# Another placement in SBUF, product f of the output projection in three passes, and a new order for a decoder layer on one core

## The chip, the cores and the metric

The kernel runs on one core of one Trainium2 chip. The metric is the device time of one execution in microseconds (us). The kernel before the change took 919.77 to 920.34 us in three runs, median 920.08. One further execution was profiled; it took 918.02 us, of which the profile's span covers 916.3.

TensorE (PE) does the matmuls: one operand is loaded into the array ("loaded", 128 x 128), the other runs through it ("streamed", 256 or 512 columns), and the result goes to a bank of PSUM. PEld is the weight load, which the profile counts apart. DVE (VectorE) and ACT (ScalarE) do the arithmetic on the vectors, POOL (GpSimd) and SP (SyncE) only start transfers here.

## The reference

One layer on 512 positions of width 1024, in float32:

```
h = rmsnorm(x)
p = h @ w_in                       # 1024 x 9216: B, C, v | a, b | queries | 3 gates
y_a = (B * conv3(C * v)) @ w_a_out
y_b = silu(layernorm(conv31(a * sigmoid(b)))) @ w_b_out
y_c = attention(queries, 256 memory tokens: K, V = rmsnorm(mem) @ w_kv) @ w_att_out
m   = sum_i sigmoid(gate_i) * y_i
x   = x + m @ w_o
x   = x + (silu(g) * up) @ w_down  # g, up = split(conv3(rmsnorm(x) @ w_up)), 2816 each
out = rmsnorm(x)
```

## The kernel before

**Precision.** Every large product is made of float32r matmuls. Each operand is split into a high part (a cast to float32r, on ACT: `whi`, `mgh`, ...) and a low part (what is left, a subtraction on DVE: `wlo`, `mgl`, ...), and three passes are added up in PSUM: high x high, high x low, low x high. Product f of the output projection (`wo_whole`, L2076) is the exception: it runs as eight full float32 matmuls on unsplit operands, which the trace records as 16.

**Quads.** The projections by `w_in`, by `w_att_out` and by `w_up` are done by a seven-product scheme on 2 x 2 blocks of 256 columns. A quad `(q, f)` is product f of group q: 24 matmuls of 256 columns (2 column halves x 4 k x 3 passes), written by `multiply` (L882). The groups are `glu` (a, b), `q`, `gate`, `cv` (C, v), `bb` (B), `mo` (attention output), `mq` and `up`. The loaded operand is the weight part, the streamed one the activation's `form`. For `mo` the streamed operand lies among the general places `lf` and `sb`, for the other groups that the prediction times in the `forms` pool. K is a quad of its own kind (`keys_product`, L1242). V, the output projection (`wo`, products a to g, of which a, b and d use weight parts held in the `forms` pool) and the down-projection (`pd`) go through `product` (L650 to L652), 512 columns each; the merge of branch b (L1832 to L1834) streams 512 columns of activations.

**Blocked matmuls.** In some quads one matmul, the first, walks its 256 columns in another order, in blocks of 16 columns taken from the two halves alternately (a "blocked" matmul, shown as `128x2x8x16`; in some `up` quads with f = 7 the block is 64, 16 or 8). Its result is the same. It stands in a quad that follows a product of 512 columns, in the listed quads of the set `FRESH`, and in these `up` quads: 35 quads in all, five of them with blocks of 64 or 8.

**Places.** SBUF holds weight parts (`wts` pool: `whi`, `wlo`, four pairs), six landing places for weights (`wf`), 6 general places `lf` from the left, 17 general places `sb` from the right, and the pool `forms`. Each place is 4096 bytes per partition. `SHIFT` is a tile of 192 bytes at the head of `forms`, so the forms start 192 bytes further than they would. The addresses that the pools give, modulo 512: weight parts 256, `lf` 256, `sb` 256, `forms` 448. The difference between the address of the streamed and of the loaded operand, modulo 512, is called the distance below: 192 in the quads whose operand is in `forms`, 0 in those of `mo`.

**Order.** A planner (`Jobs`) takes each engine's instructions as jobs with a cost, what they wait for, and what place they take. `ORDER` fixes the order of TensorE's 363 jobs. All others are put in order by due time: the time when the TensorE job that needs them is to start, less their length, plus a number by kind of job (`LATER`). `AHEAD` bounds how early a kind may run. A place is taken when free; a low part by DVE, the next addition on POOL, a landing of a weight, each follows from a due time.

**Loads.** Weights of a quad come by SP in plain transfers of 512 KB; four of the seven combinations are made by POOL transfers that add a second block onto the first as it lands. 162 such transfers run through POOL's queue.

Of the kernel before, what the change touches and what calls it, by code (L numbers as in the profile page):

```python
# [80 lines left out]
LATER = {  # L81
    "ACT c3": -1610.2, "ACT cf": -759.4, "ACT csq": -104.7, "ACT exp": -604.9,
# [29 lines left out]
    "ACT xg": 3.7, "ACT xroot": -520.5, "ACT xsq": -264.1, "ACT xsquare": -849.4,  # L112
    "ACT zh a": -212.1, "ACT zh b": -569.9, "ACT zh c": 46.3, "ACT zh d": -1022.4,
    "ACT zh e": 465.7, "ACT zh f": 365.1, "ACT zh g": -370.3, "DVE CV": -750.2, "DVE c3": -619.6,
    "DVE cf": -1.8, "DVE csum": -1543.8, "DVE ends": -15.4, "DVE fl h b00": -12.9,
# [20 lines left out]
    "DVE s6 glu": -216.7, "DVE sl": -459.1, "DVE sum": 477.6, "DVE tap 0": 173.9,  # L136
    "DVE tap 1": 446.5, "DVE tap 2": 252.4, "DVE tap 3": -27.1, "DVE top": -1718.1,
    "DVE tot1": -7.6, "DVE tot2": 42.7, "DVE um": 169.1, "DVE v scale": -86.8,
    "DVE var fold": -637.8, "DVE vl": 915.9, "DVE weigh": -3786, "DVE wl K 0": -119.6,
# [2617 lines left out]
```

## Time and profile before

| what | value |
|---|---|
| median of three runs | 920.08 us (919.77 to 920.34) |
| the profiled execution | 918.02 us |
| span of its profile | 916.3 us |
| TensorE busy | 906.6 us, 6930 records |
| DVE busy | 852.3 us, 954 instructions |
| ACT busy | 709.8 us, 992 instructions |
| POOL busy | 141.8 us, 169 instructions |
| DMA | 199.55 MB, mean 218 GB/s |

A line of engine waits gives engine, waiting instruction, what it waited for, total us, number and mean. A window gives start and end in us from the span's start, its length, then the busy time of each engine and the instructions that touch the window, the granted TensorE clock as a share of full speed, the mean busy share of the DMA engines, and GB/s. In the chain of waits a row is start, length and instruction. Dividing a window that holds only whole matmuls of one kind by their number gives the time of one.

### The profile page before, as it was taken

The numbers are of one execution on the slowest core, as the hardware profiler recorded it, in microseconds if no ns is written. First come the engines' busy times: TensorE is split into PE (matmuls) and PEld (weight loads), VectorE is DVE, ScalarE is ACT, GpSimd is POOL, SyncE is SP. The second block draws the span as 40 slices with busy tenths as digits, with TensorE's granted clock in tenths as the row PEclk, the third lists the DMA queues.
The fourth block names the chain that finished last, engine by engine and source line by source line (L and its number), as shares of the span: only waits on it lengthen the run. The fifth ranks groups of instructions, "written<-read, shape, count | busy, mean of one in ns | idle before, by whom it ended". The sixth has DMA issues, their size and how long they took to land.

```text
span 916.3 us, 17357 instructions
## 1 busy us (share of the span) xinstructions
PE 906.6 (99%) x6930; PEld 864.2 (94%) x6930; DVE 852.3 (93%) x954; ACT 709.8 (77%) x992; POOL 141.8 (15%) x169
## 2 busy tenths in 40 slices
PE   9999999999999999999999999999999999999997
PEld 8899999999999999999899997899999999988886
DVE  6997999999999999999999989897898799999987
ACT  7867989979969878799958974686777668865556
POOL 0120211011121111101111112112211211002120
PEclk9999999999999999999999999999999999999999
DMA  9998689877799869979777999999998956779972
GB/s 371 355 244 202 136 200 202 237 161 176 136 247 210 198 157 211 225 176 215 175 154 206 212 277 336 226 230 299 281 259 205 236 134 150 181 263 327 266 144 93
DMA packets 56129, 199.55 MB, mean 218 GB/s; under 512 B 6240, under 2 KB 6640, under 8 KB 56048
## 3 DMA queue, kind: packets, MB, share of 16 engines
q0 software_dynamic: 23328, 84.16, 50.5%
q1 hardware_dynamic: 32544, 114.02, 34.7%
q8 instruction: 54, 0.88, 0.4%
q10 hardware_dynamic: 176, 0.27, 0.1%
q14 instruction: 27, 0.22, 0.1%
HBM read 194.23 MB, written 4.19 MB: 217 GB/s over the span
## 4 chain that ended last, share of the span: by engine, by line
PE 95%; DVE 3%; ACT 1%; issue 1%; DVEq 0%; ACTq 0%
PE bank L882 67%; PE bank L652 6%; PE bank L650 6%; PE bank L651 6%; PE bank L1242 2%; PE bank L1833 2%; PE bank L1834 2%; PE bank L1832 2%; PE bank L2076 1%; DVE wlo L703 1%; PE bank L1111 1%; PE bank L2246 0%; PE bank L1231 0%; DVE x L2625 0%; DVE x L2604 0%
## 5 line engine op out<-in xcount | busy, mean ns | idle before, releaser
L699 ACT CAST whi<-wf 128x1024 fp32r<-128x1024 f32 x210 | 217.7, 1044 | 59.4 <-PE bank L882 32.4
L703 DVE TENSOR_TENSOR wlo<-wf,whi 128x1024 fp32r<-128x1024 f32 (+1 forms) x207 | 249.1, 1212 | 13.4 <-ACT whi L699 12.7
L1576 ACT ACTIVATE tp<-u,pk 128x510 f32<-128x510 f32 (+22 forms) x184 | 120.4, 708 | 10.5 <-DVE acc L1583 8.2
L1583 DVE TENSOR_TENSOR acc<-acc,tp 128x964 f32<-128x964 f32 (+22 forms) x92 | 109.1, 1188 | 2.7 <-ACT tp L1576 0.7
L824 POOL DMA_DIRECT2D wf<-in_w_in x52 | 47.6, 941 | 226.0 <-DVE wlo L703 180.4
L882 PE MATMUL bank<-ft4h,whi 128*128 128x256 f32 x248 | 68.8, 277 | 0.9 <-DVE V L656 0.9
L882 PE MATMUL bank<-ft6h,whi 128*128 128x256 f32 x248 | 68.9, 278 | 0.5 <-ACT bank L955 0.5
L882 PE MATMUL bank<-ft7h,whi 128*128 128x256 f32 x248 | 68.8, 277 | 0.0
L882 PE MATMUL bank<-fb11l,whi 128*128 128x256 f32 x248 | 68.7, 277 | 0.0
L882 PE MATMUL bank<-fb11h,whi 128*128 128x256 f32 x248 | 68.7, 277 | 0.0
L882 PE MATMUL bank<-fb10h,whi 128*128 128x256 f32 x248 | 68.6, 277 | 0.0
L882 PE MATMUL bank<-fb11h,wlo 128*128 128x256 f32 x248 | 68.6, 277 | 0.0
L882 PE MATMUL bank<-ft7l,whi 128*128 128x256 f32 x248 | 68.6, 277 | 0.0
L882 PE MATMUL bank<-ft4l,whi 128*128 128x256 f32 x248 | 68.6, 277 | 0.0
L882 PE MATMUL bank<-ft6l,whi 128*128 128x256 f32 x248 | 68.6, 277 | 0.0
L882 PE MATMUL bank<-ft6h,wlo 128*128 128x256 f32 x248 | 68.6, 277 | 0.0
L882 PE MATMUL bank<-ft4h,wlo 128*128 128x256 f32 x248 | 68.6, 277 | 0.0
L882 PE MATMUL bank<-ft7h,wlo 128*128 128x256 f32 x248 | 68.6, 277 | 0.0
L882 PE MATMUL bank<-fb00h,whi 128*128 128x256 f32 x248 | 68.6, 277 | 0.0
L882 PE MATMUL bank<-fb00l,whi 128*128 128x256 f32 x248 | 68.6, 277 | 0.0
L882 PE MATMUL bank<-ft5h,whi 128*128 128x256 f32 x248 | 68.6, 277 | 0.0
L882 PE MATMUL bank<-ft5l,whi 128*128 128x256 f32 x248 | 68.6, 277 | 0.0
(427 smaller groups left out, 3220.9 us busy)
## 6 DMA issues: line engine op xcount, KB each, us to landing
wf<-in_w_in SPq DMA_DIRECT2D x56, 512.0 KB, 5.0
wf<-in_w_in POOLq DMA_DIRECT2D x52, 512.0 KB, 7.5
wf<-in_w_up POOLq DMA_DIRECT2D x33, 512.0 KB, 7.2
wf<-in_w_up SPq DMA_DIRECT2D x29, 512.0 KB, 8.1
wf<-in_w_down SPq DMA_DIRECT2D x15, 512.0 KB, 4.6
wf<-in_w_v SPq DMA_DIRECT2D x8, 512.0 KB, 9.5
wf<-in_w_a_out SPq DMA_DIRECT2D x8, 512.0 KB, 5.7
wf<-in_w_b_out SPq DMA_DIRECT2D x8, 512.0 KB, 4.8
```

What stands on the lines that cost most here:

```text
L650: nc.tensor.matmul(ps, s_hi, w_hi, start=start, stop=False, skip_group_check=again)
L651: nc.tensor.matmul(ps, s_hi, w_lo, start=False, stop=False, skip_group_check=again)
L652: nc.tensor.matmul(ps, s_lo, w_hi, start=False, stop=stop, skip_group_check=again)
L699: nc.scalar.copy(parts[0], src())
L703: nc.vector.tensor_tensor(lo, src(), hi.bitcast(F32), op=ALU.subtract)
L824: nc.gpsimd.dma_start(out=tiles[key], in_=block(w, col[c], k), accum_op=ALU.add)
L882: nc.tensor.matmul(to, w[:, k, at], col, start=first and n == 0, stop=k == 3 and n == 2, skip_group_check=again,)
L1242: nc.tensor.matmul(ps[:, j, :], w[:, k, at], a[:, k, :], start=first and j == 0 and k == 0 and n == 0, stop=g == 1 and k == 3 and n == 2, ...
L1576: nc.scalar.activation(two(("tp", p, s))[:, j, s:], two(("u", p))[:, j, : SEQ - s], AF.Copy, scale=weight(j),)
L1583: nc.vector.tensor_tensor(a, a, two(("tp", p, s))[:, :, s:], op=ALU.add)
L1832: nc.tensor.matmul(ps, w_hi[:, i, at], hi, start=first, stop=False)
L1833: nc.tensor.matmul(ps, w_hi[:, i, at], lo, start=False, stop=False)
```

## The change

Six things are changed together.

1. `WO_WHOLE` is empty: product f runs as 24 float32r matmuls of 512 columns instead of eight full ones, with split operands. The program has 16 more matmuls in it and six more jobs on other engines: three casts on ACT, three subtractions on DVE.
2. The 192-byte `SHIFT` tile now heads the `lf` pool, which lies left of `forms`, so both move; `mean_col`'s tile has 72 floats instead of 56, so `sb` lies 64 bytes lower. Modulo 512 the addresses now are: weight parts 256, `lf` 448, `sb` 192, `forms` 448. The distances of the forms' quads (192) and of V (320) stay. Counting float32r matmuls by distance, the others go: `mo` (336) from 0 to 192 (160) and 448 (176); merge (192) from 0 to 192 (80) and 448 (112); the down-projection's 429 of 512 columns and 66 of 256 columns from 0 to 320; attention scores (96 of 256 columns) 40 from 0 to 256; attention output (48 of 512 columns) 36 from 0 to 256; `wo` products c, e and g (72) from 0 to 64, a, b and d (72) from 192 to 256, and f comes in at 64.
3. `LEFT_SLOTS` is 9 instead of 6. The room comes from `dynamic_dma_scratch_size`, set to 4096 bytes; before it was 16384.
4. `FRESH` is empty, and a new set `STEADY` has four quads, in which the blocked matmul is the seventh (`nth = 6`) instead of the first. Blocked matmuls stand in 23 quads in the first place and in 4 in the seventh.
5. `ORDER`, `LATER` and `AHEAD` have new numbers; in `ORDER` there is no job that was not there before, nor is one missing.
6. A new table `NUDGE` of 565 numbers moves single jobs' due times.

```diff
-WO_WHOLE = "f"
+WO_WHOLE = ""
...
-LEFT_SLOTS, RIGHT_SLOTS = 6, 17
+LEFT_SLOTS, RIGHT_SLOTS = 9, 17
...
 FRESH = {
-    (("glu", 0), 2), (("glu", 3), 5), (("glu", 3), 3), (("cv", 1), 4), (("cv", 3), 6),
-    (("bb", 1), 4), (("mq", 1), 3), (("up", 0), 6), (("up", 0), 4), (("up", 2), 6),
+
+}
+NUDGE = {
+    'ldg': -5.5, 'mfold': 227.1, 'mfold2': 36.7, 'msum': -190.7, 'rm': -137.3, 'temps': 1.2,
...
+STEADY = {
+    ('K', 2, 0), (('gate', 1, 0), 2), (('gate', 1, 0), 3), (('up', 1), 2),
 }
...
-                due[key] += LATER.get(self.kind(key), 0.0)
+                due[key] += LATER.get(self.kind(key), 0.0) + NUDGE.get(key, 0.0)
...
-    mean_col = edge.tile([P, 56], F32, tag="mean_col", name="mean_col")[:, :1]
+    mean_col = edge.tile([P, 72], F32, tag="mean_col", name="mean_col")[:, :1]
     places = {"lf": ctx.enter_context(tc.tile_pool(name="lf", bufs=1, reuse_waits="tile"))}
+    places["lf"].tile([P, SHIFT // 4], F32, tag="shift", name="shift")
     forms_pool = tc.tile_pool(name="forms", bufs=1, reuse_waits="tile")
     forms = forms_pool.__enter__()
-    forms.tile([P, SHIFT // 4], F32, tag="shift", name="shift")
...
-        run = None
-        if long_rows(seq[seq.index((q, f)) - 1]) or (q, f) in FRESH:
+        run, nth = None, 0
+        if (q, f) in STEADY:
+            run, nth = 16, 6
+        elif long_rows(seq[seq.index((q, f)) - 1]) or (q, f) in FRESH:
             run = 16
...
-                    if run is not None and (c, k, n) == (0, 0, 0):
-                        to, col = blocks(to), blocks(col)
+                    if run is not None and (c, 3 * k + n) == (0, nth):
+                        to, col = in_blocks(to, run), in_blocks(col, run)
...
+                    to, col = ps[:, j, :], a[:, k, :]
+                    if ("K", h, g) in STEADY and (j, 3 * k + n) == (0, 6):
+                        to, col = in_blocks(to, 16), in_blocks(col, 16)
...
-    nc = bacc.Bacc("TRN2", target_bir_lowering=False, num_devices=1)
+    nc = bacc.Bacc(
+        "TRN2", target_bir_lowering=False, num_devices=1, dynamic_dma_scratch_size=4096
+    )
```

The order of the instructions, at the places that the prediction speaks of. In a row, the name left of the arrow is the bank or tile that is written, the names right of it are what is read, then the shape that is streamed; "x2" is the same row twice.

TensorE in the output projection, before: one product is ending, product f stands as a full-precision pair, and the next begins (`who` parts are held weights, `mg` the merged activations).

```order
L650 MATMUL bank_6780<-whoh_6531,mgh_6593 128x512
L651 MATMUL bank_6780<-whol_6532,mgh_6593 128x512
L652 MATMUL bank_6780<-whoh_6531,mgl_6597 128x512
L2076 MATMUL bank_6799<-wo_6301,mg_6703 128x512 x2
L650 MATMUL bank_6776<-whoh_6633,mgh_6593 128x512
L651 MATMUL bank_6776<-whol_6634,mgh_6593 128x512
L652 MATMUL bank_6776<-whoh_6633,mgl_6597 128x512
```

The same place now:

```order
L830 MATMUL bank_6833<-whoh_6707,mgh_6532 128x512
L831 MATMUL bank_6833<-whol_6708,mgh_6532 128x512
L832 MATMUL bank_6833<-whoh_6707,mgl_6561 128x512
L830 MATMUL bank_6856<-whi_6703,mgh_6844 128x512
L831 MATMUL bank_6856<-wlo_6704,mgh_6844 128x512
L832 MATMUL bank_6856<-whi_6703,mgl_6849 128x512
```

Product f (bank 6856) now comes after products a and b and as three passes on parts `whi`, `wlo`, `mgh`, `mgl`.

DVE around the same place, before (L703 makes low parts of weights, L2010 and L1917 the merged activations):

```order
L2010 TENSOR_TENSOR mg_6703<-mg_6773,mg_6703 128x1024
L1917 TENSOR_TENSOR mg_6458<-g_2654,g_5777 128x512
L703 TENSOR_TENSOR whol_6796<-wo_6705,whoh_6795 128x1024
L656 SCALAR_TENSOR_TENSOR mg_6567<-mg_6703,mg_6567 128x1024
L1093 TENSOR_TENSOR wo_6705<-wo_6705,wo_6301 128x1024
```

Now:

```order
L2195 TENSOR_TENSOR mg_6743<-mg_6816,mg_6743 128x1024
L2290 TENSOR_TENSOR x_856_6676<-x_856_6676,bank_6787 128x512
L836 SCALAR_TENSOR_TENSOR mg_6596<-mg_6743,mg_6596 128x1024
L2217 TENSOR_TENSOR mgl_6849<-mg_6743,mgh_6844 128x1024
L2290 TENSOR_TENSOR x_869_6783<-x_869_6783,bank_6791 128x512
L883 TENSOR_TENSOR whol_6823<-wo_6741,whoh_6822 128x1024
```

The low part of product f's activations (`mgl_6849`, L2217) is a new row behind the sum it is made from; the low parts of its weights stand some twenty rows ahead.

TensorE at K behind the squares of the memory tokens, before: two one-column matmuls, then plain ones of 256 columns.

```order
L1242 MATMUL bank_204<-mh_127,wlo_174 128x256
L1105 MATMUL ss_247<-mean_col,msq_161 128x1 x2
L1242 MATMUL bank_252<-mh_127,whi_235 128x256
L1242 MATMUL bank_252<-ml_128,whi_235 128x256
L1242 MATMUL bank_252<-mh_127,wlo_236 128x256
```

Now the seventh matmul of that quad is blocked:

```order
L1287 MATMUL ss_247<-mean_col,msq_161 128x1 x2
L1427 MATMUL bank_252<-mh_127,whi_235 128x256
L1427 MATMUL bank_252<-ml_128,whi_235 128x256
L1427 MATMUL bank_252<-mh_127,wlo_236 128x256
...
L1427 MATMUL bank_252<-mh_127,whi_235 128x2x8x16
```

Nothing moved there but the shape of one matmul.

More of the change, by code (lines that the diff above doesn't have):

```diff
@@ L103 @@
-    "ACT tap 1": -527.4, "ACT tap 2": -125.6, "ACT tap 3": -47.1, "ACT tp 0": 7.1, "ACT tp 1": 1965,
[8 rows of a table removed]
[L112 to L115, printed above, removed]
[8 rows of a table removed]
-    "DVE kl": -1303.6, "DVE kt": -2.5, "DVE lns": -829.6, "DVE low": -328.6, "DVE m scale": -946.8,
@@ L125 @@
-    "DVE mfold": 247.7, "DVE mfold2": -512, "DVE mg0": 302.6, "DVE mgl a": 1211, "DVE mgl b": 76.2,
-    "DVE mgl c": -546.6, "DVE mgl d": -216.3, "DVE mgl e": -277.9, "DVE ml": 845.8,
[9 rows of a table removed]
[L136 to L139, printed above, removed]
[6 rows of a table removed]
@@ L146 @@
-    "DVE wsum": -13.9, "DVE x scale": -264.1, "DVE x1 a": -77.5, "DVE x1 c": -156.8,
-    "DVE x1 d": -145.7, "DVE x1 e": -1579.6, "DVE x1 f": -689.2, "DVE x1 g": 224.3, "DVE xfold": 44,
-    "DVE xn": 566.3, "DVE xnorm": -43.3, "DVE xsum": -375.3, "DVE y t4": 108.1, "DVE y t5": -139.1,
[3 rows of a table removed]
-    "NONE c3": -8.5, "NONE cf": 768.4, "NONE first tile": 4.9, "NONE mem tile": 493.4,
-    "NONE mg0 tile": 509.1, "NONE raw tile V": 505.2, "NONE rows": -498.5, "NONE sums": 35.5,
[16 rows of a table removed]
+    "ACT c3": -40.4, "ACT cf": -981.5, "ACT csq": 14.1, "ACT exp": -1786.4, "ACT fh h b00": -1117.6,
[6 rows of a table added]
@@ new lines @@
+    "ACT high": -1226.3, "ACT kh": 31.4, "ACT m root": -340.9, "ACT mg0": -158.5,
+    "ACT mgh a": -1327.1, "ACT mgh b": -211.4, "ACT mgh c": 681.3, "ACT mgh d": -494.3,
+    "ACT mgh e": 47.2, "ACT mgh f": -634.5, "ACT mgh g": -9.9, "ACT mh": 1358.2, "ACT msq": -395.6,
+    "ACT mu high": 1.6, "ACT pth": -28.4, "ACT qh": -938, "ACT r1 bb": -30.4, "ACT r1 cv": -967.1,
[8 rows of a table added]
+    "ACT rh": 66.6, "ACT rt": -111.4, "ACT sc": 339.6, "ACT sg": -1313.7, "ACT sigmoid": 2322.8,
+    "ACT silu": -82, "ACT sq": 643.4, "ACT sr": -107.5, "ACT st": -1095.6, "ACT swish": -958.9,
@@ new lines @@
+    "ACT tap 0": -324, "ACT tap 1": -223.9, "ACT tap 2": 244.3, "ACT tap 3": -501.7,
[8 rows of a table added]
+    "ACT x root": -243.3, "ACT xg": 2.3, "ACT xroot": -750.5, "ACT xsq": 159.8,
+    "ACT xsquare": -185.3, "ACT zh a": -314.8, "ACT zh b": -1201.8, "ACT zh c": -1216.5,
+    "ACT zh d": -68.9, "ACT zh e": -42.8, "ACT zh f": -683.8, "ACT zh g": 1.9, "DVE CV": -1061,
+    "DVE c3": -2765.7, "DVE centre": -234.2, "DVE cf": 1.1, "DVE csum": -331.6, "DVE ends": 149.1,
[7 rows of a table added]
+    "DVE kl": -1042.8, "DVE kt": 1592.9, "DVE lns": -357.6, "DVE low": -271.4, "DVE m scale": 473.9,
@@ new lines @@
+    "DVE mfold": -1450.4, "DVE mfold2": -2326.6, "DVE mgl a": 343.2, "DVE mgl b": -92.2,
+    "DVE mgl c": -11.4, "DVE mgl d": -18.7, "DVE mgl e": -1, "DVE mgl f": -452.3,
+    "DVE mgl g": -319.4, "DVE ml": 807.4, "DVE ms c": -205.2, "DVE ms d": 93.3, "DVE ms e": 604,
+    "DVE ms f": -753, "DVE msum": -363.3, "DVE mu fold": -566.9, "DVE mu low": -6.1,
[7 rows of a table added]
+    "DVE rd g": -1378.5, "DVE rl": -1406.4, "DVE s6 glu": 135.6, "DVE sl": -24, "DVE sum": -1070.6,
+    "DVE tap 0": -70.7, "DVE tap 1": 2098.3, "DVE tap 2": 538.9, "DVE tap 3": 497.3,
@@ new lines @@
+    "DVE top": -4186.6, "DVE tot1": -26.8, "DVE tot2": 686.9, "DVE um": 50.6, "DVE v scale": -160.4,
+    "DVE var fold": -723, "DVE var sum": -2.3, "DVE vl": 51.9, "DVE weigh": 541.2,
[9 rows of a table added]
+    "DVE xnorm": -731, "DVE xsum": 1018.3, "DVE y t4": -13, "DVE y t5": -262.8, "DVE y t6": 1501.3,
+    "DVE y t7": 30.9, "DVE ymul": -817.2, "DVE ys": 1067.8, "DVE z": -1244.6, "DVE zd": 108.8,
+    "DVE zl a": -362.1, "DVE zl b": -452.6, "DVE zl c": -1248, "DVE zl e": -117, "DVE zl f": -264.4,
+    "DVE zs c": 10, "DVE zs d": 791.7, "DVE zs e": -4.6, "NONE c3": -6, "NONE cf": -524.5,
@@ L186 @@
-    (('glu', 2), 7), (('glu', 3), 7), (('q', 0), 3), (('glu', 2), 4), (('q', 0), 2),
[3 rows of a table removed]
-    (('gate', 2, 0), 2), (('q', 1), 3), (('gate', 2, 0), 7), ('o', 0, 1), (('gate', 2, 0), 3),
[13 rows of a table removed]
-    (('cv', 3), 3), (('gate', 0, 0), 1), (('gate', 0, 1), 5), (('gate', 0, 0), 6), (('cv', 3), 2),
-    (('bb', 1), 6), (('gate', 0, 0), 7), (('gate', 0, 0), 3), (('gate', 0, 0), 2),
-    (('gate', 0, 1), 1), (('bb', 1), 7), (('gate', 0, 1), 6), (('cv', 3), 4), (('gate', 0, 1), 2),
-    (('gate', 0, 0), 4), (('gate', 0, 1), 7), (('bb', 1), 4), (('bb', 1), 3), (('gate', 0, 1), 4),
@@ L208 @@
-    (('gate', 1, 0), 5), (('gate', 0, 1), 3), (('gate', 1, 1), 5), ('merge', 0, 0, 0),
-    ('merge', 0, 1, 0), ('merge', 0, 2, 0), ('merge', 0, 0, 1), ('merge', 0, 1, 1),
-    (('gate', 1, 0), 1), ('merge', 0, 2, 1), (('gate', 1, 0), 6), (('gate', 1, 0), 3),
-    ('mu', 'mean'), (('gate', 1, 1), 1), (('gate', 1, 0), 2), (('gate', 1, 1), 6),
-    (('gate', 1, 1), 2), (('gate', 1, 0), 7), (('gate', 1, 1), 7), ('v', 'squares'),
-    (('gate', 1, 0), 4), ('v', 'rows'), ('merge', 0, 3, 0), (('gate', 1, 1), 4), ('merge', 0, 3, 1),
[29 rows of a table removed]
[3 rows of a table added]
@@ new lines @@
+    (('glu', 1), 5), (('glu', 0), 1), (('glu', 2), 5), ('K', 3, 1), (('glu', 0), 6),
+    (('glu', 1), 6), (('glu', 0), 7), (('glu', 0), 2), (('glu', 0), 3), (('glu', 0), 4),
+    (('glu', 1), 7), (('glu', 3), 5), (('glu', 2), 1), (('glu', 1), 4), (('glu', 3), 1),
+    (('glu', 1), 2), (('glu', 2), 6), (('glu', 1), 3), (('glu', 3), 2), (('q', 0), 1),
+    (('glu', 3), 6), (('q', 0), 5), (('glu', 2), 2), (('q', 0), 2), (('glu', 2), 3),
[4 rows of a table added]
+    ('s', 1, 1), (('q', 1), 2), (('gate', 2, 1), 1), (('gate', 2, 0), 7), (('gate', 2, 0), 3),
@@ new lines @@
+    ('o', 0, 1), ('o', 0, 0), ('s', 2, 0), ('s', 3, 0), ('s', 2, 1), ('s', 3, 1),
+    (('gate', 2, 0), 2), ('pt', 1, 1), (('gate', 2, 1), 6), ('pt', 1, 0), ('pt', 2, 0),
+    (('gate', 2, 1), 5), (('gate', 2, 0), 4), ('pt', 2, 1), (('gate', 2, 1), 2), ('o', 1, 1),
[11 rows of a table added]
+    (('gate', 0, 0), 1), (('bb', 1), 6), (('gate', 0, 0), 2), (('gate', 0, 0), 6),
+    (('gate', 0, 1), 1), (('bb', 1), 2), (('bb', 1), 7), (('gate', 0, 0), 7), (('bb', 1), 3),
+    (('gate', 0, 0), 3), (('gate', 0, 1), 6), (('gate', 0, 1), 2), (('gate', 0, 1), 7),
@@ new lines @@
+    (('gate', 1, 0), 5), (('gate', 0, 0), 4), (('bb', 1), 4), (('gate', 0, 1), 3),
+    (('gate', 0, 1), 4), ('merge', 0, 0, 0), ('merge', 0, 0, 1), ('merge', 0, 2, 0),
+    (('gate', 1, 1), 1), ('merge', 0, 2, 1), ('merge', 0, 1, 0), (('gate', 1, 0), 1),
+    ('merge', 0, 1, 1), (('gate', 1, 1), 5), (('gate', 1, 1), 6), ('mu', 'mean'),
+    (('gate', 1, 0), 2), (('gate', 1, 1), 7), (('gate', 1, 0), 6), (('gate', 1, 1), 2),
+    (('gate', 1, 0), 7), (('gate', 1, 1), 3), ('v', 'squares'), (('gate', 1, 0), 3), ('v', 'rows'),
@@ L243 @@
+    ('merge', 0, 3, 0), (('gate', 1, 1), 4), ('merge', 0, 3, 1), (('mq', 1), 1), (('mq', 0), 5),
[29 rows of a table added]
 ]
 AHEAD = {
[4 rows of a table removed]
-    "ACT mgh d": 20, "ACT mgh e": 20, "ACT mh": 2, "ACT msq": 5, "ACT mu high": 2, "ACT r1 bb": 2,
-    "ACT r1 cv": 40, "ACT r1 mo": 80, "ACT r1 mq": 20, "ACT r1 up": 5, "ACT r2 bb": 150,
-    "ACT r2 gate": 150, "ACT r2 glu": 40, "ACT r2 q": 150, "ACT r2 up": 150, "ACT r4 gate": 20,
-    "ACT r4 glu": 10, "ACT r4 up": 10, "ACT r5 cv": 40, "ACT r5 up": 40, "ACT r6 gate": 20,
-    "ACT r6 glu": 40, "ACT r6 mo": 150, "ACT rb": 2, "ACT rh": 5, "ACT rm": 150, "ACT silu": 150,
@@ L254 @@
-    "ACT swish": 40, "ACT tap 2": 5, "ACT tap 3": 150, "ACT tp 3": 150, "ACT v root": 80,
[9 rows of a table removed]
-    "DVE h2 t6": 40, "DVE h2 t7": 10, "DVE lns": 10, "DVE low": 2, "DVE m scale": 40,
-    "DVE mfold2": 80, "DVE mgl c": 80, "DVE mgl e": 2, "DVE ml": 40, "DVE ms c": 2,
[4 rows of a table removed]
-    "DVE sl": 40, "DVE tap 3": 150, "DVE top": 150, "DVE tot1": 80, "DVE tot2": 80,
-    "DVE v scale": 2, "DVE weigh": 5, "DVE wl K 0": 2, "DVE wl merge 0": 2, "DVE wl mix 3": 20,
[6 rows of a table removed]
-    "NONE first tile": 2, "NONE mem tile": 80, "NONE mg0 tile": 20, "NONE raw tile V": 2,
@@ L279 @@
-    "NONE rows": 80, "NONE tile": 80, "POOL ea": 20, "POOL s3 bb": 40, "POOL s3 cv": 80,
[7 rows of a table removed]
[4 rows of a table added]
+    "ACT mgh a": 10, "ACT mgh d": 20, "ACT mgh e": 150, "ACT mgh f": 40, "ACT mh": 150,
+    "ACT msq": 2, "ACT ob": 80, "ACT qh": 20, "ACT r1 bb": 150, "ACT r1 gate": 2, "ACT r1 glu": 80,
[4 rows of a table added]
+    "ACT rh": 150, "ACT rm": 80, "ACT sg": 40, "ACT silu": 150, "ACT sr": 10, "ACT swish": 5,
[4 rows of a table added]
+    "ACT wh0 V": 10, "ACT xg": 10, "ACT xroot": 10, "ACT xsquare": 20, "ACT zh a": 10,
+    "ACT zh b": 2, "ACT zh c": 2, "ACT zh d": 80, "ACT zh e": 5, "ACT zh f": 20, "ACT zh g": 150,
@@ new lines @@
+    "DVE CV": 10, "DVE c3": 40, "DVE centre": 2, "DVE csum": 20, "DVE fl h b10": 80,
[3 rows of a table added]
+    "DVE h t6": 10, "DVE h2 t4": 10, "DVE kl": 80, "DVE lns": 20, "DVE low": 20, "DVE mfold": 20,
+    "DVE mfold2": 20, "DVE mg0": 2, "DVE mgl b": 150, "DVE mgl e": 2, "DVE mgl f": 150,
+    "DVE mgl g": 20, "DVE ml": 10, "DVE ms c": 80, "DVE ms f": 20, "DVE msum": 20, "DVE mu low": 20,
[4 rows of a table added]
+    "DVE rd g": 10, "DVE rl": 10, "DVE sl": 20, "DVE sum": 80, "DVE top": 80, "DVE tot1": 2,
[4 rows of a table added]
+    "DVE xnorm": 150, "DVE y t4": 20, "DVE y t7": 80, "DVE ymul": 40, "DVE z": 2, "DVE zl a": 5,
@@ L287 @@
+    "DVE zl b": 5, "DVE zl e": 10, "DVE zl g": 2, "DVE zs e": 5, "NONE c3": 80, "NONE cf": 80,
+    "NONE mg0 tile": 80, "NONE sums": 20, "NONE temps": 2, "NONE tile": 20, "POOL ea": 80,
[9 rows of a table added]
 }
@@ L853, in quad_loads, with in_blocks @@
         split_job((q, 4), r, 4, 256, [("ld", r)], lo_from=low(4, 1, 1))
+    def in_blocks(t, run):
+        return t.rearrange("p (b two r) -> p two b r", two=2, r=run)
     def long_rows(key):
@@ L868, in multiply @@
             run = (64, 16, 8)[q[1] % 3]
-        def blocks(t):
-            return t.rearrange("p (b two r) -> p two b r", two=2, r=run)
         for c in range(2):
```

37 lines of the change are left out of this document (25 added, 12 removed), and 433 rows, old and new, of tables (AHEAD, LATER, NUDGE, ORDER).

## The prediction

> **What bounds the kernel now.** I read the busy shares first, then the slices, then TensorE's waits.
>
> ```profile
> span 916.3 us, 17357 instructions
> PE 906.6 (99%) x6930; PEld 864.2 (94%) x6930; DVE 852.3 (93%) x954; ACT 709.8 (77%) x992; POOL 141.8 (15%) x169
> PE   9999999999999999999999999999999999999997
> DVE  6997999999999999999999989897898799999987
> PE bank L2246 <- DVE mean_col L641: 0.9, 1, 0.9
> PE bank L882 <- DVE V L656: 0.9, 1, 0.9
> PE bank L882 <- ACT y L973: 0.7, 1, 0.7
> PE bank L882 <- ACT bank L955: 0.5, 1, 0.5
> PE bank L1111 <- DVE xnorm L2123: 0.4, 1, 0.4
> ```
>
> TensorE is busy in every slice up to the last. Of its waits (total, number, mean) 0.9 us is the start; the other four are 0.9 + 0.7 + 0.5 + 0.4 = 2.5 us. So the time is the sum of the durations of the matmuls, and the change is worth what it takes from them. I therefore read durations by stage: windows that lie inside a run of matmuls of one kind, with window, length, then PE, weight load, DVE, ACT and POOL busy (a count takes in the matmuls that overlap an edge), clock, DMA share and GB/s. Whole matmuls in these are 240, 168, 96, 408 and 456, all with 256 streamed columns in 24s (quads).
>
> ```profile
> 123.24:150.44 27.20, 27.20 (x243) 27.20 (x241) 27.16 (x30) 23.96 (x33) 3.99 (x5) 1.00 0.82 182
> 231.04:251.29 20.25, 20.25 (x170) 20.22 (x169) 19.45 (x20) 19.83 (x32) 3.49 (x4) 1.00 0.70 128
> 257.99:269.50 11.51, 11.51 (x98) 11.51 (x97) 11.00 (x13) 6.39 (x8) 3.51 (x4) 1.00 0.98 243
> 306.27:354.32 48.05, 48.05 (x410) 48.05 (x409) 46.07 (x48) 38.60 (x54) 8.17 (x10) 1.00 0.78 177
> 382.23:434.06 51.83, 51.83 (x457) 51.83 (x457) 51.36 (x54) 46.41 (x66) 6.05 (x7) 1.00 0.83 203
> ```
>
> The clock is 1.00 in all, and yet the rate differs: 27.20/240 = 113.3 ns, 51.83/456 = 113.7, 48.05/408 = 117.8, and in the `mo` quads (20.25 + 11.51)/264 = 120.3 ns. What sets `mo` apart is the distance from the loaded operand's address to the streamed one's, modulo 512 bytes: 0 in `mo`, 192 in the other quads. The 512-column products differ too:
>
> ```profile
> 33.20:38.70 5.50, 5.50 (x25) 4.51 (x24) 5.50 (x8) 5.50 (x8) 0.87 (x1) 1.00 1.05 304
> 439.51:461.27 21.76, 21.76 (x97) 18.02 (x96) 21.24 (x23) 16.38 (x23) 3.49 (x4) 1.00 0.73 158
> 574.00:578.20 4.20, 4.20 (x20) 3.38 (x18) 2.73 (x3) 1.30 (x2) 0.00 (x0) 1.00 1.06 275
> 832.97:843.85 10.88, 10.88 (x50) 9.01 (x49) 10.88 (x12) 5.69 (x6) 2.54 (x4) 1.00 1.06 275
> ```
>
> V (24, distance 320) 229.2 ns; merges (96, distance 0) 226.7; product d of the output projection (18, distance 192) 233.3; down-projection (48, distance 0) 226.7. So distance 0 is dear for short rows and cheap for long ones; 192 and 320 the reverse.
>
> **Product f in three passes.** Its eight full-precision matmuls stand in the chain of waits as three pieces (start, length, instruction):
>
> ```profile
> 553.37 1.72 PE bank L2076 x4
> 560.69 3.43 PE bank L2076 x8
> 571.05 1.72 PE bank L2076 x4
> ```
>
> 6.87 us go. Twenty-four float32r matmuls of 512 columns at distance 64 come: 24 x 0.231 = 5.54 us, the mean of the two apart rows (229.2, 233.3) for a distance that no row has; bounds 24 x 0.2267 and 24 x 0.2335. **-1.33** (-1.43 to -1.27). The three casts on ACT and three subtractions on DVE stand beside the PE; DVE is 153.14 busy of 162 in the stretch that ends there (row below), and 3 x 1.21 us fits in its 8.9 us of idle time. Without that cover they would cost up to 3.6 us.
>
> ```profile
> 230.00:430.00 200.00, 197.95 (x1704) 197.35 (x1703) 195.58 (x203) 170.72 (x242) 32.98 (x38) 1.00 0.85 197
> 430.00:592.00 162.00, 162.00 (x1043) 144.35 (x1042) 153.14 (x176) 119.11 (x158) 26.04 (x30) 1.00 0.88 227
> L703 DVE TENSOR_TENSOR wlo<-wf,whi 128x1024 fp32r<-128x1024 f32 (+1 forms) x207 | 249.1, 1212 | 13.4 <-ACT whi L699 12.7
> ```
>
> **Places moved.** Of the new distances 192 and 320 have rows; 448, 256 and 64 have none. My rule between the two classes: whatever isn't 0 counts as apart (short rows 113.3 ns, long ones 231), because both distances that have rows agree in kind and only 0 stands out. More rows serve:
>
> ```profile
> 906.26:908.06 1.80, 1.80 (x17) 1.79 (x15) 1.80 (x6) 1.01 (x2) 0.00 (x0) 1.00 0.00 0
> 192.55:196.86 4.31, 4.31 (x38) 4.31 (x36) 3.07 (x5) 2.44 (x7) 0.00 (x0) 1.00 1.01 203
> ```
>
> These are 15 short matmuls at the end of the down-projection (120.0 ns) and 36 of the scores (119.7), both at distance 0. Then:
> `mo`, 336 matmuls, 160 to distance 192 and 176 to 448: 336 x 7.0 ns = -2.35 (if 448 is no better, -1.12). Merges: 80 to 192 at 6.6 ns more, +0.53; 112 to 448 at 4.3, +0.48 (0 to +0.74). Down-projection, 429 long ones to 320 at 2.5 ns: +1.07; its 66 short ones to 320: 66 x 6.7 = -0.44 (0 to -0.44). Scores, 40 of 96 to 256: -0.26 (0 to -0.26). Output projection: c, e and g, 72 to 64, +0.31 (0 to +0.49); the held a, b and d, 72 from 192 to 256, -0.17 (-0.48 to 0). Attention output, 36 to 256, +0.15 (0 to +0.24). Together **-0.68**; with every unknown end good -1.9, with every one bad +1.95.
>
> [...]
>
> **The slow phase.** In the chain of waits the 0.7 us before 303.36 is followed by one long piece:
>
> ```profile
> 302.52 0.70 DVE V L656
> 303.36 64.78 PE bank L882 x552
> 17.37 0.34 PE ss L1105 x4
> 17.70 5.76 PE bank L1242 x48
> ```
>
> After the stall 18 quads ran at 117.8 ns, and the rate came back at 354.32, at the blocked first matmul of (cv 3, 6), one of the ten that the change takes out. Where the stall doesn't happen, 432 x 4.5 ns = **-1.94**. The 48 `K` matmuls behind the squares' one-column matmuls took 120.0 ns; a blocked one now stands seventh in that quad. At 113.3 they would save 0.32; the first six still come before it: **-0.25** (0 to -0.32).
>
> **Blocked starts.** 35 go to 27, counting the four moved to seventh place:
>
> ```profile
> 49.69:52.44 2.75, 2.75 (x26) 2.75 (x24) 2.75 (x3) 2.01 (x3) 0.00 (x0) 1.00 1.05 268
> 52.44:60.60 8.16, 8.16 (x75) 8.16 (x73) 8.16 (x10) 4.62 (x6) 1.76 (x2) 1.00 0.82 257
> ```
>
> The blocked quad took 2.75 us, the three behind it 2.72 each: 8 x 0.03 = **-0.2**. Ten of them may have guarded against a slow phase; that is the third rival.
>
> **Order, due times, three more places.** Between what the first `mo` quad needs and what the first merge needs, DVE now has 197 instructions instead of 201: 4 x 195.58/203 = 3.9 us less. TensorE's own work there shrinks by 2.35 + 1.94 = 4.3 us, so the 4.4 us that DVE had free in the 200 stay about 4. I take the wait on DVE (V, L656) as gone, -0.9, since its queue has less ahead of it, and the other three as they are: **-0.9** (all gone -2.5; twice as much +2.5). Loads gain nothing while TensorE doesn't wait for them.
>
> **Sum** against the profiled execution: 918.02 - 1.33 - 0.68 - 1.94 - 0.25 - 0.2 - 0.9 = 912.7 us. That execution lay 2.06 below the median of the runs, 920.08; so 914.8 us. A measurement tells 0.2%, 1.84 us, from no change: faster is below 918.24, slower above 921.92.
>
> **Rivals.**
> Shifts that cost: 448, 256 and 64 take the worse end of each, +1.95 instead of -0.68: 917.4 us. For it: no row excludes it, since most of these distances have none; against: 192 and 320 agree in kind. 0.09.
> [...]
> DVE becomes the bound: between the first `mo` quad and the first merge it has 4 us free in 200, and whatever TensorE gains beyond the 3.9 us that DVE loses there is paid back as a wait for a low part or a bank; stalls of 5.0 us instead of 1.6 give 918.2. A smaller ring for POOL's descriptors would add to it:
>
> ```profile
> q0 software_dynamic: 23328, 84.16, 50.5%
> POOL wf L824 <- DVE wlo L703: 360.3, 67, 17.3
> ```
>
> but POOL stands waiting for DVE 360 us of the span, so a slower issue has room. 0.15.
> Slower, a slow phase with no end: one stall early in `gate`, from (gate 2,1),4 to (gate 1,1),1, where the new order has some 74 quads with no blocked matmul. At 117.8 instead of 113.3 ns that is 74 x 24 x 4.5 ns = 8.0 us: 922.8 us. The gain of 5.3 is eaten from 49 quads on, and slower by 0.2% from 66. For it: the 18 quads at 303.36. Against: behind the 0.5 us wait at 382 TensorE went on at 113.7 ns. 0.09.
> Better: no stall left (-1.6) and long rows not slowed (226.7 all through, about -1): 912.2 us. 0.13.
>
> **How the numbers follow.** The forecast has the remaining 0.47, by itself 913.4 to 917.8 (stalls and shifts each half way to their bounds: -0.8 - 0.6, and 1.7 + 1.3). Faster: 0.46 + 0.08 + 0.07 + 0.06 + 0.13 = 0.80; same: 0.01 + 0.01 + 0.08 + 0.02 = 0.12; slower: 0.01 + 0.07 = 0.08, in the order forecast, costly shifts, idle shifts, DVE, endless phase, better. The range 910.8 to 920.3 leaves out most of the endless phase and a tail below the better case.
>
> **What the changed profile will show.** `mo` windows at 113.3 ns; if those to 448 stay at 120, my rule falls. Down-projection at 229 ns, product f in 5.4 to 5.6 us. No run of quads at 117.8 and a 2 us shorter stretch from 303 to 354. TensorE waits of 1.5 to 2 us without the start. Waits of 4 us or more on DVE, or long stretches at 117.8, make the prediction wrong.

## The result, and the profile after

The changed kernel took 914.22 us (median of four runs, 913.48 to 915.1); the kernel before, with the runs made beside it, 920.21. The ratio is 0.993, with a 95% interval of 0.9909 to 0.995: 0.7% faster. 914.8 was forecast. The profiled execution took 913.48 us, 4.5 us less than the profiled one of before, where the sum had 5.3.

The page of the changed kernel (span, busy times, slices) and TensorE's waits:

```profile
span 911.7 us, 17361 instructions
PE 903.9 (99%) x6938; PEld 863.1 (95%) x6938; DVE 853.0 (94%) x957; ACT 712.6 (78%) x995; POOL 142.0 (16%) x169
PE   9999999999999999999999999999999999999997
PE bank L2431 <- DVE mean_col L821: 0.9, 1, 0.9
PE bank L1413 <- ACT mg L1215: 0.4, 1, 0.4
PE bank L2438 <- DMA pk<-in_gains: 0.2, 1, 0.2
```

None of the four waits, 2.5 us together, is left. The two new ones, 0.4 and 0.2 us, stand in the first 6 us of the span. TensorE is as full as before, so the rates decide again. Windows of the changed kernel, in the columns used above; they hold 192, 672, 72, 48 and 15 whole matmuls:

```profile
232.28:254.04 21.76, 21.76 (x194) 21.76 (x193) 21.76 (x22) 21.59 (x31) 5.66 (x7) 1.00 0.78 156
286.68:362.84 76.16, 76.16 (x674) 76.16 (x673) 75.77 (x81) 61.00 (x85) 13.03 (x15) 1.00 0.89 206
425.62:442.42 16.80, 16.80 (x75) 13.54 (x73) 16.66 (x18) 16.31 (x26) 3.48 (x4) 1.00 0.97 228
838.05:849.04 10.99, 10.99 (x50) 9.02 (x48) 10.99 (x12) 6.23 (x7) 1.76 (x2) 1.00 1.06 278
901.87:903.57 1.70, 1.70 (x16) 1.70 (x15) 1.50 (x4) 1.49 (x4) 0.00 (x0) 1.00 0.07 25
```

The `mo` quads run at 21.76/192 = 113.3 ns (120.3 before), and the stretch that held the slow phase before at 76.16/672 = 113.3. The merges take 233.3 ns (226.7), the long rows of the down-projection 229.0 (226.7), its short ones 113.3 (120.0). So far the forecast holds row by row. But two other stretches are now slow; 96 and 360 whole matmuls:

```profile
153.28:164.59 11.31, 11.31 (x98) 11.31 (x97) 11.11 (x16) 11.02 (x19) 2.62 (x3) 1.00 0.96 164
505.41:547.82 42.41, 42.41 (x362) 42.41 (x360) 38.47 (x49) 37.58 (x50) 7.82 (x9) 1.00 0.94 244
```

Both give 117.8 ns. Over the whole span 32 quads run at that rate, 12 of them between the attention scores, 16 from (gate 1,1),4 to the last `mq`; before the change it was 17, and the one right behind the wait.

To see where the time went I added up, for each kind of work, the time from each TensorE matmul's start to the next one's start (so a wait counts with the work ahead of it). The last column is the experiment a_noshift, below. In us:

| work | before | changed | a_noshift |
|---|---|---|---|
| K | 21.12 | 20.77 | 20.77 |
| q and gate quads | 154.03 | 155.12 | 153.39 |
| mo quads | 41.32 | 38.08 | 40.23 |
| cv and bb quads | 117.28 | 114.24 | 114.33 |
| merges | 43.68 | 44.87 | 43.68 |
| mq quads | 38.12 | 39.58 | 38.10 |
| output projection | 40.20 | 38.77 | 38.88 |
| transposes behind it | 3.92 | 3.25 | 3.25 |
| up quads | 209.82 | 209.76 | 210.75 |
| down-projection | 105.66 | 105.84 | 105.43 |
| the rest | 133.94 | 134.23 | 133.67 |
| sum | 909.09 | 904.51 | 902.48 |

### The profile page after: what moved, and what is told of

It is laid out like the page before. It is cut to its first block, busy times and chain, and to the rows that moved or that the text cites. A ratio compares the mean times of both kernels' runs of the same rounds, so it can differ in the third digit from the quotient of the medians.

```text
span 911.7 us, 17361 instructions
## 1 busy us (share of the span) xinstructions
PE 903.9 (99%) x6938; PEld 863.1 (95%) x6938; DVE 853.0 (94%) x957; ACT 712.6 (78%) x995; POOL 142.0 (16%) x169
## 4 chain that ended last, share of the span: by engine, by line
PE 99%; DMA 0%; ACT 0%; DVE 0%; issue 0%; DVEq 0%; ACTq 0%
PE bank L1064 69%; PE bank L832 7%; PE bank L831 7%; PE bank L830 7%; PE bank L1427 2%; PE bank L2019 2%; PE bank L2018 2%; PE bank L2017 2%; PE bank L1293 1%; DMA first<-in_first 0%; PE bank L1413 0%; PE ss L1287 0%; PE rows L1293 0%; ACT mg L1215 0%; DVE x L2810 0%
## 5 line engine op out<-in xcount | busy, mean ns | idle before, releaser
L879 ACT CAST whi<-wf 128x1024 fp32r<-128x1024 f32 x189 | 196.8, 1045 | 61.9 <-PE bank L1064 25.3
L883 DVE TENSOR_TENSOR wlo<-wf,whi 128x1024 fp32r<-128x1024 f32 x186 | 223.4, 1211 | 12.9 <-ACT whi L879 12.7
L1768 DVE TENSOR_TENSOR acc<-acc,tp 128x1004 f32<-128x1004 f32 (+22 forms) x92 | 109.1, 1188 | 1.9 <-ACT tp L1761 0.6
L1004 POOL DMA_DIRECT2D wf<-in_w_in x45 | 40.4, 898 | 207.4 <-DVE wlo L883 161.4
L1064 PE MATMUL bank<-fb00h,wlo 128*128 128x256 f32 x248 | 68.8, 277 | 0.0
L1064 PE MATMUL bank<-fb10h,wlo 128*128 128x256 f32 x248 | 68.7, 277 | 0.0
L1064 PE MATMUL bank<-fb10l,whi 128*128 128x256 f32 x248 | 68.7, 277 | 0.0
```

Source lines behind the costliest of these rows:

```text
L879: nc.scalar.copy(parts[0], src())
L883: nc.vector.tensor_tensor(lo, src(), hi.bitcast(F32), op=ALU.subtract)
L1004: nc.gpsimd.dma_start(out=tiles[key], in_=block(w, col[c], k), accum_op=ALU.add)
L1064: nc.tensor.matmul(to, w[:, k, at], col, start=first and n == 0, stop=k == 3 and n == 2, skip_group_check=again,)
L1768: nc.vector.tensor_tensor(a, a, two(("tp", p, s))[:, :, s:], op=ALU.add)
```

## The experiments

The theory after the result: two things are at work in the places. A distance of 0 costs short rows 7 ns and spares long ones up to 6.6. Beside that there is a lasting slow phase, in which quads run at 117.8 ns until a blocked matmul ends it; what begins one is a wait, or rows that run at another rate than in the kernel before. The rivals: the slow stretches come from traffic beside TensorE, or from the new order.

**Blocked matmuls put into the slow stretches of the changed kernel (a_steady).**

```diff
 STEADY = {
     ('K', 2, 0), (('gate', 1, 0), 2), (('gate', 1, 0), 3), (('up', 1), 2),
+    (('gate', 2, 0), 5), (('q', 0), 4), (('q', 1), 3), (('q', 1), 2), (('gate', 2, 0), 2),
+    (('gate', 1, 1), 6), (('mq', 0), 5),
 }
```

> The changed kernel with the blocked matmul in seventh place in seven more quads: (gate 2,0),5, (q 0),4, (q 1),3, (q 1),2, (gate 2,0),2, (gate 1,1),6 and (mq 0),5. These stand where quads run at 117.8 ns instead of 113.3. Theory: the slow phase is a lasting relation between streams and weight loads, and a blocked matmul behind the first six ends it: 28 quads at 2.83 us go back to 2.72, 28 x 0.11 = 3.1 us less some 0.5 us for the blocked rows: 911.6 us against 914.2. Rival: the quads are slow for something that lasts through them (DMA, DVE or ACT traffic): then nothing is gained, 914.2 to 914.5 us, and they still show 117.8 ns.

912.29 us (911.3 to 913.02); ratio to before 0.992, interval 0.9899 to 0.9942. Windows of it, 24 matmuls of (mq 1),1, whose first is blocked, and the 168 behind (mq 0),5, whose seventh is:

```profile
505.23:508.06 2.83, 2.83 (x26) 2.83 (x24) 2.83 (x6) 2.22 (x4) 0.00 (x0) 1.00 1.05 204
510.82:529.86 19.04, 19.04 (x170) 19.04 (x169) 16.18 (x21) 18.02 (x26) 4.38 (x5) 1.00 0.94 220
```

117.9 ns, and then 113.3, with the DMA share at 0.94 as in the slow stretch of the changed kernel. So the rate doesn't follow the traffic; DVE and ACT are about as busy in both, too (16.18 and 18.02 of 19.04 us here, 38.47 and 37.58 of 42.41 there). Here a blocked matmul in first place did not end the phase that began in the merge ahead of it, and one in seventh place did. All the quads aimed at are at 113 ns; four elsewhere are slow, and 13 others, from (bb 1),2 to (gate 0,1),4, which were at 113.3 in the changed kernel, ran at 117.8 in this trace: a slow phase had begun where no blocked matmul stands. These 13 cost 1.4 us in this trace. The time alone doesn't tell this kernel from the changed one (0.992 and 0.993, with intervals that overlap); the rates of the quads do.

**The places put back (a_noshift), and the places alone (b_shift).** The first is the changed kernel, the second the one before with the opposite edit.

```diff
-    mean_col = edge.tile([P, 72], F32, tag="mean_col", name="mean_col")[:, :1]
+    mean_col = edge.tile([P, 56], F32, tag="mean_col", name="mean_col")[:, :1]
...
-    places["lf"].tile([P, SHIFT // 4], F32, tag="shift", name="shift")
...
     forms = forms_pool.__enter__()
+    forms.tile([P, SHIFT // 4], F32, tag="shift", name="shift")
```

> The changed kernel with the places as they were before (192 bytes ahead of the forms, not ahead of the left places; right places 64 bytes higher); orders and due times stay. Theory: by distance alone mo loses 2.2 us, merges gain 1.2, the down-projection 0.6, the output projection 0.3, scores lose 0.3: 0.4 us slower; but the slow phases behind the scores and behind the merges were brought by the new distances and go, 32 quads x 0.11 = 3.5 us: 911.1 us. Rival: the slow phases come with the new order, whatever the places: 914.6 us.

911.49 us (911.07 to 913.32); ratio 0.9918 (0.9892 to 0.9944). Windows of it: seven `mo` quads (168), two of the merges (48), the 13 `mq` and `gate` quads (312) that were slow:

```profile
230.52:250.66 20.14, 20.14 (x170) 20.14 (x169) 19.67 (x20) 19.17 (x27) 4.84 (x6) 1.00 0.77 148
431.55:442.43 10.88, 10.88 (x50) 9.01 (x48) 10.74 (x13) 10.83 (x18) 0.88 (x1) 1.00 1.06 232
507.02:542.38 35.36, 35.36 (x315) 35.36 (x313) 32.72 (x42) 33.38 (x44) 6.97 (x8) 1.00 0.96 248
```

`mo` is back at 119.9 ns, the merges at 226.7, and no quad of the whole span is slow. The order and the due times are those of the change to the last job, so these 32 slow quads came with the places, not with the order.

> The kernel before with the moved places alone (192 bytes ahead of the left places, right places 64 bytes lower). Theory: the distances bring -2.2 (mo), +1.2 (merges), +0.6 (down-projection), -0.3 (scores) and 0.3 (output projection), -0.4 us in all, and the new slow phases behind scores and merges come with them, some 20 quads x 0.11 = 2.2 us more; the stall at 303 and its slow phase stay: 922 us against 920.2. Rival: no new slow phase, 919.8 us.

920.25 us (919.1 to 921.61) against 919.39 for the kernel before; ratio 1.0011 (0.9997 to 1.0025), no difference that can be told. Its trace shows 49 slow quads instead of 17, among them the `mq` quads (264 matmuls here):

```profile
512.78:543.88 31.10, 31.10 (x267) 31.10 (x266) 27.23 (x34) 27.53 (x36) 6.97 (x8) 1.00 0.99 244
```

117.8 ns, with the old order. What the moved places save in `mo` is eaten there too: 2.2 us less in `mo`, 1.2 more in the merges, 32 quads x 0.11 = 3.5 more in slow phases. The theory had 922; the 17 slow quads at 306 went, and 12 came at 382, behind the wait there. Not all of the 49 are the places' doing: these 12 and five in `up` are slow in the trace of b_wo (below) as well, where no place is moved. The other 32 stand among the scores, among the merges and from (gate 1,1),4 to the end of `mq`. In those stretches every trace with moved places has slow phases; in the eight traces with no place moved (the kernel before, a_noshift, noshift_again, a_moblock, a_best, b_nofresh, b_wo, b_ring4) none begins there that is longer than a single quad.

**Both again, side by side (after_again, noshift_again)**, since the first two had been timed on different chips.

> The changed kernel once more, beside the two that follow, since the 2.7 us between it and the kernel with no place moved were measured on different chips. Theory: the moved places cost it 2 to 3 us net (32 slow quads, merges, down-projection, against mo): 2 to 3 us above the next kernel. Rival: the difference was the chip's: within 1 us of it.

> The changed kernel with the places as before, once more. Theory: no slow quads, 2 to 3 us below the changed kernel. Rival: within 1 us.

915.43 us and 912.24 us; ratios to before (920.81 here) 0.9941 (0.9919 to 0.9962) and 0.9906 (0.9884 to 0.9928). 3.2 us lie between the medians; the two intervals overlap by a little, but both pairs of measurements agree, 2.7 and 3.2. In the trace of the first the same 32 quads are slow, from the same jobs to the same jobs; in that of the second none. So the moved places took away some 3 us of what the rest of the change brought.

**Only the right places moved (a_sb).**

```diff
-    places["lf"].tile([P, SHIFT // 4], F32, tag="shift", name="shift")
...
     forms = forms_pool.__enter__()
+    forms.tile([P, SHIFT // 4], F32, tag="shift", name="shift")
```

> The changed kernel with only the right places moved (64 bytes lower); left places where they were before. Theory: slow phases come from long rows and scores whose operands lie apart, so moving a part of the places brings a part of them; by distance it differs from the kernel with no place moved by -1.2 (176 mo matmuls) +0.7 (112 of the merges) +0.4 (output projection), about 0; with some 10 to 20 slow quads more: 912.5 to 913.7 us. Rival: one kind of place alone brings the phases: 911.4 if the left ones, 915 if the right ones.

916.39 us (914.47 to 918.44); ratio 0.9955 (0.9939 to 0.9971), no better than the whole move. 59 quads ran at 117.8 ns in its trace, that of the slowest of its ten runs; 14 of them are in `up`, where the changed kernel has none. Two windows: two `mo` quads (48 matmuls) whose operand lies on the left throughout, at distance 0; then six `mo` quads and two of `cv` (192):

```profile
240.45:246.21 5.76, 5.76 (x51) 5.76 (x50) 5.56 (x6) 5.20 (x8) 0.00 (x0) 1.00 0.77 171
246.21:268.82 22.61, 22.61 (x194) 22.61 (x193) 21.40 (x22) 19.91 (x27) 6.13 (x7) 1.00 0.89 195
```

So the right places alone are enough to bring the phases, nearer to the rival; the left ones alone were not tried. The first window gives 120.0 ns, as at distance 0 elsewhere. The second gives 117.8: `mo` quads at 448, which take 113.3 in the changed kernel, are in a slow phase here, and those that mix 0 and 448 run at 117.8 with them. So the rate depends on what ran ahead and not on the distance alone.

**FRESH emptied in the kernel before (b_nofresh).**

```diff
 FRESH = {
-    (("glu", 0), 2), (("glu", 3), 5), (("glu", 3), 3), (("cv", 1), 4), (("cv", 3), 6),
-    (("bb", 1), 4), (("mq", 1), 3), (("up", 0), 6), (("up", 0), 4), (("up", 2), 6),
 }
```

> The kernel before with the set FRESH empty: ten blocked starts fewer, nothing else. Theory: a slow phase lasts until a blocked matmul ends it; the one that begins behind the stall at 303 now goes past (cv 3,6) at 354 up to the merges at 434, 29 quads x 0.11 = 3.2 us more, less 10 x 0.03: 922.3 us against 919.4. Rival: the blocked matmuls do nothing and phases end of themselves: 919.1 us, with the same 17 or 18 slow quads.

923.74 us (918.54 to 927.45) against 921.47 beside it; ratio 1.0024 (1.0004 to 1.0045). In its trace the phase that begins behind the wait at 302 lasts 46 quads (1104 matmuls), to the merges, and another 32 quads (768) in the `up` stage:

```profile
308.99:439.02 130.03, 130.03 (x1107) 130.03 (x1106) 126.22 (x132) 109.21 (x152) 19.42 (x23) 1.00 0.83 196
608.09:698.55 90.46, 90.46 (x771) 90.46 (x770) 76.16 (x81) 64.38 (x82) 17.59 (x21) 1.00 1.01 257
```

117.8 ns both. The blocked matmul of (cv 3),6 had ended the first of them in the kernel before; without it the phase doesn't end of itself. The phase in `up` tells the same: in the traces of b_shift, b_wo and b_ring4 it begins at the same quad, (up 0),2, and ends six quads on, where (up 0),6 has its blocked matmul. Here it goes on past (up 3),7, whose first matmul walks in blocks of 64, and ends at (up 4),7, whose first walks in blocks of 16. The runs of this kernel lie 9 us apart, those of the kernel before 5, as they would if not every execution had these phases; only one was traced, the slowest of the ten (927.45).

**Product f alone (b_wo)**: `WO_WHOLE` emptied in the kernel before.

```diff
-WO_WHOLE = "f"
+WO_WHOLE = ""
```

> The kernel before with product f in three float32r passes, nothing else (the planner places six more jobs). Theory: the eight full matmuls cost 5.7 us and the first matmul behind each of three pieces 0.4 us more; 24 x 0.2267 = 5.4 us come: 918.0 us against 919.4. Rival: the three casts and three subtractions come late in a stretch in which DVE is 95% busy, and a wait of 1.4 us or more takes the gain: 919.4 us or more.

936.77 us (933.68 to 938.41); ratio 1.0179 (1.0147 to 1.0211): 15 us slower. TensorE's waits in it, and two windows of 15 us, which hold the waits of 4.6 and of 4.5 us:

```profile
PE bank L652 <- DVE mgl L2032: 4.6, 1, 4.6
PE bank L650 <- ACT whi L699: 4.5, 1, 4.5
PE bank L650 <- ACT mgh L2027: 3.8, 1, 3.8
PE bank L2246 <- DVE mean_col L641: 0.9, 1, 0.9
PE bank L651 <- DVE wlo L703: 0.9, 1, 0.9
...
560.00:575.00 15.00, 10.37 (x37) 7.74 (x36) 12.60 (x12) 3.80 (x5) 3.52 (x4) 0.71 1.04 355
590.00:605.00 15.00, 9.57 (x34) 7.18 (x33) 7.66 (x10) 7.27 (x11) 0.00 (x0) 0.77 0.18 71
```

The casts and subtractions that the three passes need come 4 us late each under the old order and due times, and the mean granted clock falls to 0.71 and 0.77. What TensorE saves, 1.4 us, was had only with the new order and due times; no other way to place the six jobs was tried.

**Six left places instead of nine (a_slots6).**

```diff
-LEFT_SLOTS, RIGHT_SLOTS = 9, 17
+LEFT_SLOTS, RIGHT_SLOTS = 6, 17
```

> The changed kernel with 6 left places instead of 9, the small descriptor scratch as in the change. Theory: TensorE never waits for a load, so the places are worth nothing while the due times hold: within 1 us of 914.2. Rival: the missing waits (2.5 us of them before the change) are the work of the three places; without them a weight lands late, and 2 us or more of waits come back: 916.5 us or more.

949.6 us (948.25 to 951.11); ratio 1.0327 (1.0304 to 1.0351). The waits of TensorE:

```profile
PE bank L1064 <- DVE wlo L883: 12.9, 8, 3.6
PE bank L832 <- DVE mgl L2217: 3.6, 1, 3.6
PE bank L1064 <- ACT whi L879: 1.7, 1, 1.7
```

The theory is wrong by far: the new order and due times need the nine places. This doesn't give the worth of three places as such, since the planner puts all other engines' work in another order when places are short; it says that the two belong together.

**The small descriptor scratch alone (b_ring4)**: `dynamic_dma_scratch_size=4096` in the kernel before.

> The kernel before with the descriptor scratch of 4096 bytes instead of 16384, nothing else. Theory: POOL spends most of the span waiting for DVE, so a smaller ring holds nothing up: within 0.2% of the kernel before, POOL busy 142 us as before. Rival: POOL transfers are issued later, and waits for weights cost 1 us or more.

921.28 us (918.78 to 923.96) against 920.81; ratio 1.0001 (0.9986 to 1.0015), POOL busy 141.7 us. Nothing is lost by it.

The trace also shows what a wait does to the rate. Behind a wait of 0.5 us at 385 it goes on at 113.3 ns, as the kernel before does at 382; in b_wo, behind the same wait at 383, the same 12 quads (288 matmuls) are slow. First b_wo, then b_ring4:

```profile
386.23:420.15 33.92, 33.92 (x290) 33.92 (x289) 32.57 (x33) 30.58 (x45) 3.46 (x4) 1.00 0.74 185
388.05:420.69 32.64, 32.64 (x291) 32.64 (x289) 31.66 (x32) 29.22 (x44) 3.45 (x4) 1.00 0.73 182
```

So such a wait is followed by a slow phase in one execution and not in another. Beside the phase at 306, b_ring4 has 11 slow quads that the trace of the kernel before has not, at 109 and 603 us: single traces of nearly the same work differ by a microsecond or more in this.

**Every `mo` matmul blocked (a_moblock)**, on the kernel with no place moved.

```diff
+        if q[0] == "mo":
+            run, nth = 16, None
-        if (q, f) in STEADY:
+        elif (q, f) in STEADY:
...
-                    if run is not None and (c, 3 * k + n) == (0, nth):
+                    if run is not None and (nth is None or (c, 3 * k + n) == (0, nth)):
```

> The changed kernel with no place moved, and all 336 mo matmuls blocked (16 columns of each half in turn). Theory: at distance 0 the streamed address stays in step with the loaded one; the blocked walk takes it out of step, and mo goes from 120 to 113 to 116 ns: 1.3 to 2.2 us less than without, 909.3 to 910.2 us. Rival: the blocked walk itself costs, and every matmul takes 120 ns or more: 911.5 us or more.

913.26 us (911.49 to 914.01); ratio 0.9924 (0.9899 to 0.995). Its `mo` window, 168 matmuls:

```profile
230.88:251.04 20.16, 20.16 (x170) 20.16 (x169) 19.67 (x20) 19.21 (x27) 4.84 (x6) 1.00 0.75 151
```

120.0 ns: a blocked walk in place of a plain one, throughout, neither cures distance 0 nor costs anything; the rival holds. Whether such a quad would end a slow phase isn't shown, since none of these stood in one. This trace has 16 slow quads with no place moved: three in `up`, and the same 13 as in a_steady, here 312 matmuls at 117.8 ns:

```profile
391.37:428.12 36.75, 36.75 (x315) 36.75 (x313) 36.02 (x38) 31.02 (x43) 2.60 (x3) 1.00 0.76 205
```

So the moved places are not the only thing that brings slow phases. Just ahead of the 13, in (gate 0,1),1, TensorE is held up for some 0.2 us; it is so in a_noshift and a_best too, and no phase follows there.

**No place moved, and two blocked matmuls more (a_best)**, in seventh place in (cv 3),6 and (bb 1),2.

```diff
-    ('K', 2, 0), (('gate', 1, 0), 2), (('gate', 1, 0), 3), (('up', 1), 2),
+    ('K', 2, 0), (('gate', 1, 0), 2), (('gate', 1, 0), 3), (('up', 1), 2), (('cv', 3), 6), (('bb', 1), 2),
```

> The changed kernel with the places as before and a blocked matmul in seventh place in (cv 3),6 and (bb 1),2. Theory: a slow phase that begins by chance in the stretch from 340 to 430 us, where no other blocked matmul stands, ends there; in an execution with no such phase two blocked rows cost 0.06 us: 0 to 1 us below the kernel without. Rival: a blocked row costs more than it saves: slower by 0.2 us or more.

912.83 us (911.47 to 916.11); ratio 0.9911 (0.9889 to 0.9933), beside 0.9906 without them: no difference that can be told. Its trace has no slow quad either. The kernel with no place moved is 0.8 to 0.9% below the one before; none of those tried is measurably faster.

## Why the prediction was right

The time and its direction were right, 914.8 forecast and 914.22 measured. Term by term, in us, from the table of kinds of work and the windows:

| term | forecast | measured |
|---|---|---|
| product f | -1.33 | -1.35 |
| places moved, by distance | -0.68 | -0.5 |
| slow phase, with the blocked starts | -2.14 | +1.3 |
| K behind the squares | -0.25 | -0.35 |
| waits, with the matmuls that restart behind them | -0.9 | -3.2 |
| the rest | 0 | -0.4 |
| sum | -5.3 | -4.5 |

The measured ones are worked out so. Places: `mo` 336 x 6.7 ns = -2.2, merges +1.2, down-projection 429 x 2.3 ns - 66 x 6.7 ns = +0.55, output projection beside product f -0.1. Waits: what is left of the change in `mo` (-1.0), -0.7 in the transposes behind the output projection, -1.1 in `cv` and -0.7 in `gate` where the waits at 303 and 382 stood, and +0.3 at the start. Slow phases: what is left in `cv` and `bb` (-1.9), in q and `gate` (+1.8) and in `mq` (+1.5). The rest is mostly the down-projection, where the windows give +0.55 and the table +0.18. All of it compares two single executions.

- **Product f.** Its 24 passes take 5.52 us, 230 ns each, where 231 was taken between two rows. This window of the changed kernel holds twelve:

```profile
561.54:564.30 2.76, 2.76 (x13) 2.25 (x12) 2.76 (x5) 0.51 (x1) 0.00 (x0) 1.00 1.04 209
```

The casts and subtractions lay beside TensorE as forecast. The price named for the case without that cover, 3.6 us, was far too small: b_wo paid 13 us of waits and a lower clock. DVE's idle time in a stretch doesn't say that the new work falls into it; the order does.

- **Places.** The rule that any distance but 0 counts as apart held for 448: `mo` is at 113.3 ns there as it is at 192. Within the long rows 448 is like 192 (all merges 233.3), where 231 had been taken. Down-projection 229.0 and 113.3 as forecast. For short rows at 256 the rule failed: the scores gained nothing (11.53 and 11.57 us). This window of the changed kernel holds eleven of them, eight at 256 and three at 0:

```profile
147.57:148.89 1.32, 1.32 (x13) 1.32 (x12) 1.32 (x3) 1.23 (x2) 0.00 (x0) 1.00 0.95 251
```

1.32/11 = 120.0 ns. The chances give 0.07 to idle shifts; no run shows all rates unmoved by the places, and a_noshift shows the contrary most plainly: there the same `mo` quads take 119.9 ns instead of 113.3 for their place alone.

- **The slow phase is the step that failed.** "Where the stall doesn't happen, -1.94": the stall didn't happen and that stretch is clean, but 32 other quads run at 117.8 ns. I had read a stall as the cause; it is neither needed nor enough. In the changed kernel phases begin behind scores and behind merges with no wait near, and a_noshift and b_shift show that the moved places bring them. Thus the places, -0.5 us by distance, cost 2.7 to 3.2 us in all. The mechanism was in the forecast as the rival of 0.09, in which a phase doesn't end for want of a blocked matmul; b_nofresh shows that mechanism at work, with up to 46 quads. Its place was wrong: the 74 quads of `cv`, `bb` and `gate` stayed clean in the changed kernel's trace; 13 of them are slow in those of a_steady and a_moblock.

- **Waits** made up for it. -0.9 was taken, since only one of four waits was thought gone. All four went, and with them the time in which TensorE restarts behind a wait (the quad at 303.36 took 2.90 us, the ones behind it 2.83), which hadn't been counted. What brought this is the new order with its due times and the three places together; a_slots6 shows that they don't work apart, and the part of each stays open.

- **DVE as the bound** did not come: it is busy 853.0 us, 852.3 before, and but for the start TensorE doesn't wait for it. The smaller descriptor scratch cost nothing (b_ring4, 921.28 us against 920.81).

So two terms were missed by more than 2 us each in opposite directions, and the total came out right in part by chance.

What stays open: how a slow phase begins, and why a blocked matmul ends it. The traces show that it depends on what runs ahead, that behind the same wait it may come or not, that it lasts (up to 46 quads in b_nofresh), and that the clock (1.00) and the DMA share (0.94 in the changed kernel's slow stretch at 505 and in a_steady's clean one at 511) are the same inside and outside.
